# Residues of gate columns by VectorE in two blocks, and one more plain unit ahead of a pair in two places, in a hybrid attention/convolution block with SwiGLU

## The chip, the cores and the metric

The kernel runs on one core of one Trainium2 chip. The metric is device time in microseconds (us) of one execution, the median of several runs. Times inside an execution come from a hardware profile of one execution; they count from the start of its span.

The engines are TensorE (PE, matrix products; its weight loads are listed apart as PEld), VectorE (DVE), ScalarE (ACT), GpSimd (POOL) and SyncE (SP). SP does nothing here but issue loads; POOL issues the DMAs that add to what lies at their target.

## The reference, cut to what matters

All is float32, 256 tokens, width 2048, hidden width of the feed-forward part 5632.

```python
xn = rms_norm(h, norm1_g[l])
proj = jnp.einsum('bsd,dn->bsn', xn, w_in[l].astype(xn.dtype))
...
h = h + jnp.einsum('bsm,md->bsd', mixed, w_out[l].astype(mixed.dtype))
hn = rms_norm(h, norm2_g[l])
a = jnp.einsum('bsd,df->bsf', hn, w_gate[l].astype(hn.dtype))
bu = jnp.einsum('bsd,df->bsf', hn, w_up[l].astype(hn.dtype))
h = h + jnp.einsum('bsf,fd->bsd', jax.nn.silu(a) * bu, w_down[l].astype(hn.dtype))
```

What is left out (differential attention and a causal depthwise convolution with its norms) runs in the first 300 us and isn't touched. The change lies in the last three lines.

## The kernel before

**Products in three parts.** A float32 product is made of rounded halves: each operand is split into a rounded value (hi) and its residue (lo), and hi·hi, lo·hi and hi·lo are added up. For a weight tile `raw` that means a cast `whi` on ScalarE (L322) and a residue `wlo = raw - whi`. The residue is made in one of two ways. On VectorE it is one subtraction (L331). By DMA, ScalarE writes the negated rounded value to `wlo` (L325), and POOL issues a transfer that adds `raw` to it in place (L326), 512 KB each.

**Blocks and passes.** The hidden width is cut into 11 column blocks of 512 (j = 0 to 10), in groups of 4, 4 and 3. Behind each group comes a pass of `w_down` over the group's rows, as two double columns of 2 x 512. So the order is: block 0, blocks 1 to 3, pass; blocks 4 to 7, pass; blocks 8 to 10, pass. Block 0 is done plainly. Every other block, and every double column of a pass, is a list of units that share eight PSUM banks:

- **g** and **u**, plain units: two 128-row tiles of the gate (or up) columns, 12 matmuls of 128x512. In a pass, g and u are the left and right columns of a double column. First half: eight matmuls with `whi` (L1011, L1012). Second half: four with `wlo` (L1017).
- **s**, a pair: two row tiles of both gate and up columns as a 2x2 block product with seven products instead of eight, so 21 matmuls (L990, L991, L992). Its sums of weights are made on VectorE (L963, L964, L965), rounded on ScalarE (L966, L969), and the residues come from VectorE (`wlb` L972, `wlt` L973). The first L992 of a pair reads `wlt`, which is made last.

A block has four pairs and four units each of g and u. `BY_DMA` names the plain units whose residue is made by DMA: the first two g and the second and fourth u of a block. Block 1 has none of the g.

**Order.** A string gives each block's units: `ORDER` for blocks 2 to 10, `FIRST_ORDER` for block 1, `DORDERS` for the passes (by the number of blocks in the group, one string for each double column). `run_chunks` walks through the units. Near a pair it loads and rounds a unit three units ahead of TensorE, makes its residue two ahead, and loads a pair's weights six ahead. Everything else (sums of the banks L1091 to L1096, adding up a finished block or pass L1110 and L1151, transposes) is a generator that is taken one step further at fixed points within the units. So an engine's queue is fixed when the program is built, and each engine works strictly in that order; moving one letter of a string moves work on every engine.

Buffers: five of `raw`, three each of `whi` and `wlo`, two of a pair's weights `wb`. A load is issued by SP in the order of the program and waits there for its buffer, and what is behind it waits too.

**Names.** Below, "the first pair of block 4" is the first s of its string. Block 1 runs from 393.5 to 437 us, block 4 from 605.9 to 650.6, block 8 from 861.2 to 906.3, the last double column of the last pass from 1022.2 to the end.

Of the kernel before, what the change touches and what calls it, by code (L numbers as in the profile page):

```python
# [77 lines left out]
BY_DMA = dict(g=TWOS[:2], u=TWOS[1::2])  # L78

ORDER = "sggsggsuusuu"  # L80
FIRST_ORDER = "gsgsggsuusuu"


HD = N // P
ND = 2
DORDERS = {4: ("gguuggsguugsuu", "sgggugggusuuuu"), 3: ("gguusggsuu", "ggsggsuuuu")}

Q1, Q6, Q7, Q5, Q2, Q4, Q3, QX = range(8)

# [7 lines left out]
FIRSTS = [sum(FGROUPS[: g + 1]) for g in range(len(FGROUPS))]  # L97
# [13 lines left out]
def tile_block(  # L111
# [925 lines left out]
    def fast_block(order, pairs, twos, sources, operands, half, whole, by_dma=dict(g=(), u=())):  # L1037

        units, sums = [], {}
        left = dict(s=list(pairs), g=list(twos), u=list(twos))  # L1040
        for kind in order:
            what = left[kind].pop(0)
            c = dict(kind=kind, sums=sums, done=None, first={}, last={}, rows=what["rows"], **operands)
            if kind == "s":
                c.update(p=what["p"], load=lambda c: None, round=round_pair, split=split_pair, multiply=multiply_pair,
                         uses=[q for q, _, _ in PRODUCTS])
                c["from"] = sources
            else:
                w, col = sources[kind]
                c.update(ks=what["ks"], w=w, nk=2, width=N, cols=[(col, N)], by_dma=what["k"] in by_dma[kind],  # L1050
                         load=load_chunk, round=round_chunk, split=split_chunk, multiply=multiply_two,
                         uses=(Q3, QX) if kind == "u" else (Q2, Q4))
            units.append(c)
        assert not any(left.values())
        for q in range(8):
            users = [c for c in units if q in c["uses"]]
            users[0]["first"][q] = users[-1]["last"][q] = True
        [c for c in units if c["kind"] != "u"][-1]["done"] = half
        units[-1].update(done=whole, prompt=True)
        chunks.extend(units)  # L1060

    def gate_up_block(j):
        fast_block(ORDER if j > 1 else FIRST_ORDER, [dict(p=p, rows=slice(p, p + HK + 1, HK)) for p in range(NS)],
                   [dict(ks=ks, rows=slice(ks[0], ks[1] + 1, ks[1] - ks[0]), k=ks) for ks in TWOS],
                   dict(g=(w_gate, j * N), u=(w_up, j * N)),
                   dict(pairs=lambda: forms.get("pair"), plain=lambda k: forms["plain"][k]),
                   products_done, lambda sums: block_done(j, sums),
                   BY_DMA if j > 1 else dict(g=(), u=BY_DMA["u"]))

    def down_pass(g, j0, nb):  # L1070
        k0 = j0 * HD
# [2 lines left out]
                for a, b in zip(ks[::2], ks[1::2])]  # L1074
        for i, order in enumerate(DORDERS[nb]):
            n = 2 * i
# [28 lines left out]
    def block_done(j, q):  # L1105
        while "g" not in halfway:
            yield
        g, u = halfway.pop("g"), halfway.pop("u")
        for m, i in enumerate((Q3, QX)):
            dve.tensor_tensor(u[m], q[i], u[m], ALU.add)  # L1110
        for m in range(NM):
            dve.tensor_tensor(u[m], u[m], g[m], ALU.mult)
        yield from lag(4)
        yield from transposed(j, u)
# [74 lines left out]
    for g, nb in enumerate(FGROUPS):  # L1189
        for j in range(j0, j0 + nb):  # L1190
            if j:
                gate_up_block(j)
                continue

            block(w_gate, j * N, range(KD), fh, silu_done)
            block(w_up, j * N, range(KD), fh, lambda ps, j=j: up_done(j, ps))
            chunks[-1]["prompt"] = True
        down_pass(g, j0, nb)
        j0 += nb
# [33 lines left out]
```

## Time and profile before

| | us |
|---|---|
| median of three runs (lowest, highest) | 1063.49 (1062.6, 1063.9) |
| the profiled execution's own time | 1060.47 |
| its span | 1058.7 |
| share of the chain of work that ended last: TensorE, VectorE, DMA | 83%, 7%, 3% |

By stretch of the span, the busy time of each engine, the granted clock and the mean busy share of the 16 DMA engines (block 4 and block 8 are the first and third row, the blocks behind them the second and fourth):

```profile
606.00:656.00 50.00, 46.78 (x208) 38.05 (x207) 41.44 (x41) 28.85 (x26) 6.28 (x8) 1.00 0.98 280
656.00:698.00 42.00, 42.00 (x191) 34.77 (x190) 37.68 (x36) 27.79 (x26) 3.47 (x4) 1.00 0.83 250
861.00:911.00 50.00, 47.56 (x203) 38.90 (x202) 41.22 (x40) 29.14 (x26) 6.60 (x8) 0.97 0.98 280
911.00:954.00 43.00, 43.00 (x198) 35.60 (x196) 38.67 (x37) 28.19 (x27) 3.46 (x4) 1.00 0.83 247
```

The columns behind the stretch are its length and the busy us of PE, PEld, DVE, ACT and POOL, each with its number of instructions, then clock, DMA share and GB/s. In the two blocks that come first in a group TensorE has idle time and the DMA engines have hardly any; in the blocks behind them it is the other way round.

### The profile page before, as it was taken

How to read it: one execution, taken by the hardware profiler on the slowest of the kernel's cores; microseconds unless marked ns; L12 is line 12 of the kernel's file. 1: busy time of each engine (PE TensorE's matmuls, PEld its weight loads, DVE VectorE, ACT ScalarE, POOL GpSimd, SP SyncE). 2: the span in 40 equal slices, each digit the busy share in tenths (PEclk: the TensorE clock that was granted, in tenths of full speed). 3: DMA queues.
4: the chain of work that ended last, by engine and by line, in shares of the span. 5: the costliest groups of instructions: out<-in, count | busy, mean ns of one | idle time of the engine just before them, and what ended most of it. 6: DMA issues, size and time to landing. Idle time of an engine off the chain costs nothing.

```text
span 1058.7 us, 13117 instructions
## 1 busy us (share of the span) xinstructions
PE 1042.8 (99%) x4702; PEld 857.3 (81%) x4702; DVE 892.2 (84%) x1087; ACT 626.3 (59%) x802; POOL 104.5 (10%) x147
## 2 busy tenths in 40 slices
PE   9999999999999999999999989999999999999998
PEld 7888888877888777888888878888888878888876
DVE  5799989899666699899687888989878788889896
ACT  6644567755766565676453656666654456667442
POOL 0030122211100100000001100000000110010010
PEclk9999999999999999999999999999999999999999
DMA  9755555553546566987857698879856889798692
GB/s 300 232 179 194 199 171 171 176 170 133 176 171 226 183 228 205 292 254 223 250 186 226 202 293 246 266 207 277 259 172 226 237 209 295 211 296 251 173 280 95
DMA packets 123470, 231.33 MB, mean 219 GB/s; under 512 B 7956, under 2 KB 25806, under 8 KB 123404
## 3 DMA queue, kind: packets, MB, share of 16 engines
q1 hardware_dynamic: 113904, 201.61, 56.3%
q0 software_dynamic: 9440, 28.84, 14.0%
q8 instruction: 37, 0.61, 0.2%
q14 instruction: 29, 0.24, 0.1%
q10 hardware_dynamic: 60, 0.03, 0.0%
HBM read 202.14 MB, written 9.44 MB: 200 GB/s over the span
## 4 chain that ended last, share of the span: by engine, by line
PE 83%; DVE 7%; DMA 3%; issue 3%; ACT 2%; POOL 2%; DVEq 0%; POOLq 0%; ACTq 0%
PE q L1017 11%; PE q L1011 11%; PE q L1012 11%; PE acc L367 9%; PE acc L362 9%; PE acc L361 9%; PE q L992 7%; PE q L990 7%; PE q L991 7%; DVE wlo L331 2%; DMA wlo<-raw 2%; DVE y L512 1%; PE ps_a L828 1%; ACT whi L322 1%; PE ps_o L724 1%
## 5 line engine op out<-in xcount | busy, mean ns | idle before, releaser
L322 ACT CAST whi<-raw 128x1024 fp32r<-128x1024 f32 x272 | 282.6, 1051 | 162.9 <-PE acc L362 56.7
L331 DVE TENSOR_TENSOR wlo<-raw,whi 128x1024 fp32r<-128x1024 f32 x234 | 283.7, 1225 | 87.5 <-ACT whi L322 85.6
L969 ACT CAST wh<-wt 128x2048 fp32r<-128x2048 f32 x52 | 99.6, 1915 | 63.4 <-DVE wt L965 62.9
L973 DVE TENSOR_TENSOR wlt<-wt,wh 128x2048 fp32r<-128x2048 f32 x52 | 119.1, 2290 | 15.0 <-ACT wh L969 14.7
L361 PE MATMUL acc<-whi,xhi 128*128 128x512 f32 x320 | 126.3, 395 | 0.5 <-ACT whi L322 0.5
L1011 PE MATMUL q<-whi,chi 128*128 128x512 f32 x320 | 125.7, 393 | 0.0
L362 PE MATMUL acc<-whi,xlo 128*128 128x512 f32 x320 | 125.0, 391 | 0.2 <-DVE xlo L236 0.2
L1012 PE MATMUL q<-whi,clo 128*128 128x512 f32 x320 | 124.8, 390 | 0.0
L990 PE MATMUL q<-wh,fhi 128*128 128x512 f32 x280 | 109.9, 393 | 0.0
L991 PE MATMUL q<-wh,flo 128*128 128x512 f32 x280 | 109.0, 389 | 0.0
L512 DVE SCALAR_TENSOR_TENSOR y<-upad,cw,y 128x256 f32<-128x256 f32 x240 | 102.8, 490 | 0.0
L1011 PE MATMUL q<-whi,ahi 128*128 128x512 f32 x256 | 100.2, 391 | 0.0
L1012 PE MATMUL q<-whi,alo 128*128 128x512 f32 x256 | 99.7, 389 | 0.0
L972 DVE TENSOR_TENSOR wlb<-wb,wh 128x1536 fp32r<-128x1536 f32 x52 | 91.1, 1753 | 5.3 <-ACT wh L966 5.3
L1017 PE MATMUL q<-wlo,chi 128*128 128x512 f32 x320 | 86.8, 393 | 5.7 <-DMA wlo<-raw 5.7
L367 PE MATMUL acc<-wlo,xhi 128*128 128x512 f32 x320 | 87.7, 396 | 0.9 <-DVE wlo L331 0.8
L966 ACT CAST wh<-wb 128x1536 fp32r<-128x1536 f32 x52 | 76.7, 1474 | 0.0
L1017 PEld LDWEIGHTS q<-wlo,chi 128*128 128x128 f32 x320 | 60.3, 189 | 19.3 <-DMA wlo<-raw 6.9
L326 POOL DMA_DIRECT2D wlo<-raw x38 | 32.8, 864 | 402.0 <-ACT wlo L325 209.5
L361 PEld LDWEIGHTS acc<-whi,xhi 128*128 128x128 f32 x320 | 60.1, 188 | 13.5 <-ACT whi L322 0.8
L362 PEld LDWEIGHTS acc<-whi,xlo 128*128 128x128 f32 x320 | 60.1, 188 | 13.2 <-DVE xlo L236 1.0
L1011 PEld LDWEIGHTS q<-whi,chi 128*128 128x128 f32 x320 | 60.4, 189 | 12.5
(229 smaller groups left out, 1782.4 us busy)
## 6 DMA issues: line engine op xcount, KB each, us to landing
raw<-in_w_down_dram SPq DMA_DIRECT2D x64, 512.0 KB, 7.4
raw<-in_w_in_dram SPq DMA_DIRECT2D x48, 512.0 KB, 4.6
raw<-in_w_gate_dram SPq DMA_DIRECT2D x48, 512.0 KB, 7.2
raw<-in_w_up_dram SPq DMA_DIRECT2D x48, 512.0 KB, 6.4
wb<-in_w_up_dram SPq DMA_DIRECT2D x40, 512.0 KB, 3.8
wb<-in_w_gate_dram SPq DMA_DIRECT2D x40, 512.0 KB, 5.0
wlo<-raw POOLq DMA_DIRECT2D x38, 512.0 KB, 6.8
raw<-in_w_in_dram SPq DMA_DIRECT2D x64, 256.0 KB, 5.6
```

The source lines that it names most:

```text
L322: act.copy(c["hi"], c["raw"])
L331: dve.tensor_tensor(c["lo"], c["raw"], c["hi"].bitcast(F32), ALU.subtract)
L361: pe.matmul(ps[m], xhi[:, ms], hi[:, j, :], start=c["first"] and j == 0, stop=False)
L362: pe.matmul(ps[m], xlo[:, ms], hi[:, j, :], start=False, stop=False)
L367: pe.matmul(ps[m], xhi[:, ms], lo[:, j, :], start=False, stop=c["last"] and j == nk - 1)
L512: dve.scalar_tensor_tensor(y[:, ct, :], src, wk, y[:, ct, :], ALU.mult, ALU.add)
L973: dve.tensor_tensor(lot, c["t"], c["hi"][:, :SUMMED].bitcast(F32), ALU.subtract)
L990: pe.matmul(ps, hi, c["hi"][:, w], start=bool(first), stop=False)
L991: pe.matmul(ps, lo, c["hi"][:, w], start=False, stop=False)
L1011: pe.matmul(ps, xs[i][0][:, ms], hi[:, i, :], start=i == 0 and bool(c["first"].get(qs[m])), stop=False)
L1012: pe.matmul(ps, xs[i][1][:, ms], hi[:, i, :], start=False, stop=False)
L1017: pe.matmul(sum_bank(c, qs[m]), xs[i][0][:, ms], lo[:, i, :], start=False, stop=i == 1 and bool(c["last"].get(qs[m])))
```

## The change

Three edits. The g units of the first block behind a pass (blocks 4 and 8; `FIRSTS` holds 4, 8 and 11) get their residues from VectorE instead of DMA. In block 1 the third g moves ahead of the second pair. In the second double column of the last pass the third g moves ahead of the first pair.

```diff
-FIRST_ORDER = "gsgsggsuusuu"
+FIRST_ORDER = "gsggsgsuusuu"
...
-DORDERS = {4: ("gguuggsguugsuu", "sgggugggusuuuu"), 3: ("gguusggsuu", "ggsggsuuuu")}
+DORDERS = {4: ("gguuggsguugsuu", "sgggugggusuuuu"), 3: ("gguusggsuu", "gggsgsuuuu")}
...
-                   BY_DMA if j > 1 else dict(g=(), u=BY_DMA["u"]))
+                   BY_DMA if j > 1 and j not in FIRSTS else dict(g=(), u=BY_DMA["u"]))
```

VectorE's queue at the start of block 4, from the last up unit's residue of the pass on, before:

```order
L331 TENSOR_TENSOR wlo<-raw,whi 128x1024
L972 TENSOR_TENSOR wlb<-wb,wh 128x1536
L973 TENSOR_TENSOR wlt<-wt,wh 128x2048
L1151 TENSOR_TENSOR sum_5407<-q_5209,sum_5407 128x512
L1151 TENSOR_TENSOR sum_5409<-q_5274,sum_5409 128x512
L963 TENSOR_TENSOR wt<-wb 128x1024
L964 TENSOR_TENSOR wt<-wb,wt 128x512
L965 TENSOR_TENSOR wt<-wt,wb 128x512
L972 TENSOR_TENSOR wlb<-wb,wh 128x1536
L973 TENSOR_TENSOR wlt<-wt,wh 128x2048
```

and of the change:

```order
L331 TENSOR_TENSOR wlo<-raw,whi 128x1024
L972 TENSOR_TENSOR wlb<-wb,wh 128x1536
L973 TENSOR_TENSOR wlt<-wt,wh 128x2048
L331 TENSOR_TENSOR wlo<-raw,whi 128x1024
L1151 TENSOR_TENSOR sum_5407<-q_5209,sum_5407 128x512
L1151 TENSOR_TENSOR sum_5409<-q_5274,sum_5409 128x512
L331 TENSOR_TENSOR wlo<-raw,whi 128x1024
L963 TENSOR_TENSOR wt<-wb 128x1024
L964 TENSOR_TENSOR wt<-wb,wt 128x512
L965 TENSOR_TENSOR wt<-wt,wb 128x512
L972 TENSOR_TENSOR wlb<-wb,wh 128x1536
L973 TENSOR_TENSOR wlt<-wt,wh 128x2048
```

The two new L331 stand on either side of the pass's last sums, and the second pair's work (L963 to the last L973) is behind both. At the same place ScalarE loses two L325 and POOL two L326. Block 8 reads alike.

VectorE's queue in block 1, from behind block 0's products (the second and third pair are the two groups of L963 to L973), before:

```order
L331 TENSOR_TENSOR wlo<-raw,whi 128x1024
L963 TENSOR_TENSOR wt<-wb 128x1024
L964 TENSOR_TENSOR wt<-wb,wt 128x512
L965 TENSOR_TENSOR wt<-wt,wb 128x512
L972 TENSOR_TENSOR wlb<-wb,wh 128x1536
L973 TENSOR_TENSOR wlt<-wt,wh 128x2048
L331 TENSOR_TENSOR wlo<-raw,whi 128x1024 x2
L963 TENSOR_TENSOR wt<-wb 128x1024
```

and of the change:

```order
L331 TENSOR_TENSOR wlo<-raw,whi 128x1024 x2
L963 TENSOR_TENSOR wt<-wb 128x1024
L964 TENSOR_TENSOR wt<-wb,wt 128x512
L965 TENSOR_TENSOR wt<-wt,wb 128x512
L972 TENSOR_TENSOR wlb<-wb,wh 128x1536
L973 TENSOR_TENSOR wlt<-wt,wh 128x2048
L331 TENSOR_TENSOR wlo<-raw,whi 128x1024
L963 TENSOR_TENSOR wt<-wb 128x1024
```

One residue moved from behind the second pair to in front of it. On TensorE a whole plain unit and a group of four transposes (L828) moved in front of that pair; on SP one load of gate weights moved ahead of its `wb`.

VectorE's queue at the start of the last double column (the L1096 belongs to the one before; the first pair is L963 to the first L973), before:

```order
L1096 TENSOR_TENSOR sum_8654<-q_8443,sum_8654 128x512
L963 TENSOR_TENSOR wt<-wb 128x1024
L964 TENSOR_TENSOR wt<-wb,wt 128x512
L965 TENSOR_TENSOR wt<-wt,wb 128x512
L331 TENSOR_TENSOR wlo<-raw,whi 128x1024
L1151 TENSOR_TENSOR sum_8653<-q_8498,sum_8653 128x512
L1151 TENSOR_TENSOR sum_8655<-q_8501,sum_8655 128x512
L972 TENSOR_TENSOR wlb<-wb,wh 128x1536
L973 TENSOR_TENSOR wlt<-wt,wh 128x2048
L331 TENSOR_TENSOR wlo<-raw,whi 128x1024 x2
L963 TENSOR_TENSOR wt<-wb 128x1024
```

and of the change:

```order
L1096 TENSOR_TENSOR sum_8650<-q_8439,sum_8650 128x512
L331 TENSOR_TENSOR wlo<-raw,whi 128x1024
L1151 TENSOR_TENSOR sum_8649<-q_8494,sum_8649 128x512
L1151 TENSOR_TENSOR sum_8651<-q_8497,sum_8651 128x512
L963 TENSOR_TENSOR wt<-wb 128x1024
L964 TENSOR_TENSOR wt<-wb,wt 128x512
L965 TENSOR_TENSOR wt<-wt,wb 128x512
L331 TENSOR_TENSOR wlo<-raw,whi 128x1024
L972 TENSOR_TENSOR wlb<-wb,wh 128x1536
L973 TENSOR_TENSOR wlt<-wt,wh 128x2048
L331 TENSOR_TENSOR wlo<-raw,whi 128x1024
L963 TENSOR_TENSOR wt<-wb 128x1024
```

The first pair's work moved behind the two L1151, which add the last sums of the double column before; the second pair now follows with one residue between them instead of two.

## The prediction, made before the changed kernel ran

> **What bounds the kernel now.** First the page, for the engine that sets the time, then the view of waits of that engine:
>
> ```profile
> PE 1042.8 (99%) x4702; PEld 857.3 (81%) x4702; DVE 892.2 (84%) x1087; ACT 626.3 (59%) x802; POOL 104.5 (10%) x147
> ```
> ```profile
> PE q L1017 <- DMA wlo<-raw: 5.7, 3, 3.0
> PE q L992 <- DVE wlt L973: 1.9, 2, 1.0
> ```
>
> TensorE is busy 99% of the span, and nothing in the change alters what it multiplies. So the only time to be had is what TensorE spends waiting or running slowly. The two largest entries are the two that the change aims at: a plain unit's third products (L1017) waiting for a residue made by DMA, and a pair's third matmul (L992) waiting for VectorE. The timeline of TensorE shows where. Block 4 (columns: start, length, both us; the bracket is idle time before and who ended it):
>
> ```profile
> 610.70 0.39 PE L1011 MATMUL q<-whi,chi 128*128 128x512 f32 x1
> ...
> 615.71 1.20 PE L1017 MATMUL q<-wlo,chi 128*128 128x512 f32 x4 [3.03 <-DMA wlo<-raw]
> ...
> 619.94 0.39 PE L990 MATMUL q<-wh,fhi 128*128 128x512 f32 x1
> ```
>
> Block 8:
>
> ```profile
> 866.04 0.39 PE L1011 MATMUL q<-whi,chi 128*128 128x512 f32 x1
> ...
> 870.46 2.07 PE L1017 MATMUL q<-wlo,chi 128*128 128x512 f32 x4 [2.44 <-DMA wlo<-raw]
> ...
> 875.71 0.39 PE L990 MATMUL q<-wh,fhi 128*128 128x512 f32 x1
> ```
>
> The second pair of block 1, and the last pass:
>
> ```profile
> 404.57 0.39 PE L990 MATMUL q<-wh,fhi 128*128 128x512 f32 x1
> 404.79 0.39 PE L991 MATMUL q<-wh,flo 128*128 128x512 f32 x1
> 406.21 0.50 PE L992 MATMUL q<-wlt,fhi 128*128 128x512 f32 x1 [1.03 <-DVE wlt L973]
> 406.55 0.40 PE L990 MATMUL q<-wh,fhi 128*128 128x512 f32 x1
> ```
> ```profile
> 1027.63 0.39 PE L990 MATMUL q<-wh,dhi 128*128 128x512 f32 x1
> 1027.86 0.39 PE L991 MATMUL q<-wh,dlo 128*128 128x512 f32 x1
> 1029.13 0.50 PE L992 MATMUL q<-wlt,dhi 128*128 128x512 f32 x1 [0.88 <-DVE wlt L973]
> ...
> 1033.57 0.39 PE L1011 MATMUL q<-whi,ahi 128*128 128x512 f32 x1
> ...
> 1039.01 0.39 PE L990 MATMUL q<-wh,dhi 128*128 128x512 f32 x1
> ```
>
> Undisturbed matmuls start 0.227 us apart. The last two rows give a yardstick: two plain units take 1039.01 - 1033.57 = 5.44 us, so one takes 2.72 (first half 1.81, second 0.91), and a pair (21 matmuls) about 4.77. A pair wants its first residue 0.45 us after its start.
>
> **Blocks 4 and 8: the residues.** What goes is, in each block, two negated casts on ScalarE (L325) and two accumulating transfers of 512 KB. What comes is two subtractions (L331) on VectorE. Between the start of the first gate unit and the next pair block 4 takes 619.94 - 610.70 = 9.24 us, block 8 875.71 - 866.04 = 9.67 us. At the yardstick both take 5.44. So **3.80 us** and **4.23 us** are to be had, if nothing else is late.
>
> Part of the second sum is clock. Behind a wait of 2.44 us four matmuls took 2.07 us, where the four behind the longer wait of block 4 took 1.20. The unit's eighth matmul started at 866.04 + 7 x 0.227 = 867.63, so the wait itself is 870.46 - 867.63 less one step, 2.6 us. The other 1.6 us are that half speed. The Trainium skill ("TensorE: Matmul & The Clock Gate", Part 1) states that the array drops to half clock after an idle window of about 3.4 us and that the window runs freely. Here the gap of 2.44 us was followed by half speed and that of 3.03 us was not, so length alone does not decide. I take the trace (one of two), with none and both as bounds: 1.6 us either way.
>
> Is anything else late? VectorE's queue in block 4:
>
> ```profile
> 603.82 2.28 DVE L973 TENSOR_TENSOR wlt<-wt,wh 128x2048 fp32r<-128x2048 f32 x1
> 606.02 1.28 DVE L1151 TENSOR_TENSOR sum<-q,sum 128x512 f32<-128x512 f32 x2
> 607.22 1.21 DVE L963 TENSOR_TENSOR wt<-wb 128x1024 f32<-128x1024 f32 x1
> ...
> 611.87 2.29 DVE L973 TENSOR_TENSOR wlt<-wt,wh 128x2048 fp32r<-128x2048 f32 x1 [0.31 <-ACT wh L969]
> ```
>
> The new L331 of the first gate unit runs at 606.02, where L1151 stood; its rounded half was cast before (ScalarE loses work here). It is done by 607.2; TensorE wants it at 610.70 + 1.81 = 612.5. The second runs behind L1151, done by 609.6, wanted at 615.2. Neither is waited for. What queues behind them is the second pair: L963, L964, L965, ScalarE's cast L969, L973. An L331 takes 1.13 us of the queue (1023.92 - 1022.79 in the rows of the last pass, below), so all of it moves by 2.27 us: L973 ends at 611.87 + 2.29 + 2.27 = 616.43. The pair now starts at 610.70 + 5.44 = 616.14 and wants it at 616.59. **Margin 0.16 us**: I cost it at nothing; the bound is 0.4 us a block, should the casts or the semaphores come a little later. Block 8 is the same picture with the same margin: its L973 ended at 869.50, becomes 871.77, wanted at 866.04 + 5.44 + 0.45 = 871.93.
>
> ```profile
> 867.21 2.29 DVE L973 TENSOR_TENSOR wlt<-wt,wh 128x2048 fp32r<-128x2048 f32 x1 [0.31 <-ACT wh L969]
> ```
>
> The third pair is freer. Its chain follows the second's end by two L331 and 6.94 us (L963's start to L973's end, 607.22 to 614.16): 616.3 + 2.27 + 6.94 = 625.5, wanted at 616.14 + 4.77 + 5.44 + 0.45 = 626.8. That holds if the fourth gate unit's weights land by 616; the DMA view from 600 to 660 us speaks for it:
>
> ```profile
> q0 software_dynamic: 1424, 4.16, 37.4%
> ```
>
> The queue with the accumulating transfers took 37.4% of 60 us on all 16 engines for 4.16 MB, 5.4 us a MB. Two residues are 1.05 MB: 5.6 us of all engines go from the busiest stretch.
>
> SP's queue moves too: the fourth pair's weights are issued when L972 of the second is done, now 2.27 us later, and the first two up units' behind them. More on that among the rivals.
>
> **Block 1: a plain unit in front of the second pair.** TensorE wanted L992 at 404.57 + 0.45 = 405.02 and had it at 406.21; the next step was 0.34 instead of 0.227. Together **1.30 us**. Afterwards the pair starts one unit (2.72) and one group of transposes later, while the extra L331 in front of its chain costs 1.13, so its residue is there at 406.15 + 1.13 = 407.3, wanted after 407.7. The third pair's chain hardly moves, as the L331 only changed sides and L839 now stands behind it: its L973 ends near 415.3, wanted near 415.7. L992 of the first pair still waits its 0.2 us. On SP a gate load is now ahead of the second pair's weights and holds them until its buffer is free; they are used some 8 us later. I cost these at nothing, bound 0.3.
>
> **The last pass: three gate units first.** Here VectorE is the bound, and the gain is not the whole wait:
>
> ```profile
> 1020.21 1.22 DVE L963 TENSOR_TENSOR wt<-wb 128x1024 f32<-128x1024 f32 x1
> ...
> 1022.79 1.22 DVE L331 TENSOR_TENSOR wlo<-raw,whi 128x1024 fp32r<-128x1024 f32 x1
> 1023.92 1.28 DVE L1151 TENSOR_TENSOR sum<-q,sum 128x512 f32<-128x512 f32 x2
> 1025.12 1.75 DVE L972 TENSOR_TENSOR wlb<-wb,wh 128x1536 fp32r<-128x1536 f32 x1
> 1026.79 2.29 DVE L973 TENSOR_TENSOR wlt<-wt,wh 128x2048 fp32r<-128x2048 f32 x1
> 1028.99 2.35 DVE L331 TENSOR_TENSOR wlo<-raw,whi 128x1024 fp32r<-128x1024 f32 x2
> ```
>
> The two L1151 now stand ahead of the pair's L963, and they wait for TensorE's last unit of the pass before. That unit ends where the first gate unit starts, 1027.63 - 5.44 = 1022.19; its four third products start at 1021.28, and the first sum is complete after two of them: 1021.28 + 0.23 + 0.39 = 1021.9. From there: two L1151 (1.20), L963 to L965 (1022.79 - 1020.21 = 2.58), L331 (1.13), L972 (1026.79 - 1025.12 = 1.67), L973 (2.29): 1021.95 + 8.87 = 1030.82. The pair now starts at 1027.63 + 2.72 = 1030.35 and wants it at 1030.80: a wait of about 0.1 us with the slow step, so it ends near 1030.87 + 4.44 = 1035.3 (4.44 as from 1029.13 to 1033.57). The next pair follows after one unit only: start 1038.0, wanted at 1038.5. Its chain is L973's slot (1028.99 - 1026.79 = 2.20), one L331 (1.13) and 6.94 us behind 1028.54: 1038.8. Wait 0.4 us, with the slow step 0.5. It ends at 1038.85 + 4.44 = 1043.3, against 1039.01 + 4.77 = 1043.8 before. **0.5 us** gained of 1.15; bounds 0 and 1.15. Behind it the same four up units follow.
>
> **Sum.** 3.8 + 4.2 + 1.3 + 0.5 = 9.8 us off the profiled execution: span 1058.7 to 1048.9, its own time 1060.47 to 1050.7. The median of the runs shown is 1063.49, 3.0 us more than that execution; the same difference gives 1053.7 us.
>
> **Rivals.** (1) The clock: typical runs may not have the half-speed stretch, as block 4 had none. Then 1.6 us of the sum do not exist: 1055.3. For it: only one wait of the two had it. By the free-running window of the Trainium skill ("TensorE: Matmul & The Clock Gate", Part 1) it would be a matter of chance in each run. Chance 0.18.
>
> (2) The wait moves to the next residue by DMA, the second up unit's. TensorE wants that at 616.14 + 4.77 + 5.44 + 4.77 + 2.72 + 1.81 = 635.7 now. Its DMA can be issued only when ScalarE has cast it, behind the third pair's L969: by my estimate near 626.6. Landing times of the four residues from 600 to 640 us:
>
> ```profile
> DMA to landing us min/median/max: 5.8/8.3/11.7
> ```
>
> At the median it lands at 634.9, at the longest at 638.3: a wait of 2.6 us. Twice that is 5.2: 1058.9. Against it: the long ones are the two that go. Chance 0.10.
>
> (3) The change swaps one wait for another: VectorE's chain comes not 0.2 but several us late at the second and third pairs of blocks 4 and 8. It would need about 2 us at each of the four to bring the gain under 0.2% (2.1 us), and the queue worked out above has that only if L969's cast were delayed as well. Time 1062. Chance 0.04.
>
> (4) Slower: SP's queue. The first two up units' weights were issued from here on, now 2.27 us later:
>
> ```profile
> 612.57 3.48 SPq L317 DMA_DIRECT2D raw<-in_w_up_dram  x2
> ```
>
> The first must be cast before TensorE reaches it at 631.1, so it must land by 630, 15.2 us after an issue at 614.8. Each us beyond is lost in both blocks. The time passes 1063.49 + 2.1 when landing takes over 21 us, 1.8 times the longest above; at 22 us it is 1067.3. Chance 0.03.
>
> **How the numbers follow.** Forecast 0.65, rivals 0.18, 0.10, 0.04, 0.03. Low end: half speed behind both waits (-1.6), the last pass in full (-0.65), and 1 us for the three that the runs take beyond the profiled one: 1050.5. High end: no half speed (+1.6), nothing in the last pass (+0.5), both blocks' bound (+0.8), block 1's (+0.3), and some of rival 2: 1057.5. Against 0.2%, about what a measurement of this kernel can tell from no change, faster has 0.93, same 0.04, slower 0.03.
>
> **What would show it.** In the changed profile the waits of L1017 for DMA should be gone; blocks 4 and 8 should take 5.4 to 5.9 us from the first gate unit to the second pair; L992 of block 1's second pair should not wait; in the last pass both pairs should wait, together about half a microsecond. The forecast is wrong if L992 waits over 0.5 us in blocks 4 or 8, or if L1017 waits for the up unit's residue.

## The result, and the profile after

| | before | changed |
|---|---|---|
| median of the runs (lowest, highest), us | 1063.05 (1062.09, 1063.9) | 1051.05 (1050.87, 1051.5) |
| the profiled execution's own time, us | 1060.47 | 1051.14 |
| its span, us | 1058.7 | 1049.4 |

The ratio is 0.9888, with a 95% interval of 0.9871 to 0.9905: 12.0 us gained, 1053.7 us forecast, 1051.05 measured. The changed kernel's four runs lie within 0.6 us of each other, those of before within 1.8.

The view of TensorE's waits from 380 us on (who waited for whom; us in total, times, longest) has one row left:

```profile
PE q L992 <- DVE wlt L973: 0.2, 1, 0.2
```

The waits for a residue by DMA are gone. The timeline of TensorE at the first gate unit and the second pair of block 4, and of block 8 (start, length, us):

```profile
609.42 0.39 PE L1011 MATMUL q<-whi,chi 128*128 128x512 f32 x1
...
614.86 0.39 PE L990 MATMUL q<-wh,fhi 128*128 128x512 f32 x1
615.09 0.39 PE L991 MATMUL q<-wh,flo 128*128 128x512 f32 x1
615.32 0.39 PE L992 MATMUL q<-wlt,fhi 128*128 128x512 f32 x1
```
```profile
861.20 0.39 PE L1011 MATMUL q<-whi,chi 128*128 128x512 f32 x1
...
866.64 0.39 PE L990 MATMUL q<-wh,fhi 128*128 128x512 f32 x1
866.86 0.39 PE L991 MATMUL q<-wh,flo 128*128 128x512 f32 x1
867.09 0.44 PE L992 MATMUL q<-wlt,fhi 128*128 128x512 f32 x1
```

Both stretches take 5.44 us, in place of 9.24 and 9.67. VectorE's queue in block 4 with the two new L331 to either side of L1151:

```profile
602.54 2.28 DVE L973 TENSOR_TENSOR wlt<-wt,wh 128x2048 fp32r<-128x2048 f32 x1
604.75 1.22 DVE L331 TENSOR_TENSOR wlo<-raw,whi 128x1024 fp32r<-128x1024 f32 x1
605.88 1.28 DVE L1151 TENSOR_TENSOR sum<-q,sum 128x512 f32<-128x512 f32 x2
607.08 1.22 DVE L331 TENSOR_TENSOR wlo<-raw,whi 128x1024 fp32r<-128x1024 f32 x1
608.21 1.22 DVE L963 TENSOR_TENSOR wt<-wb 128x1024 f32<-128x1024 f32 x1
...
612.87 2.29 DVE L973 TENSOR_TENSOR wlt<-wt,wh 128x2048 fp32r<-128x2048 f32 x1 [0.32 <-ACT wh L969]
```

L973 ends at 615.16 and TensorE reads it at 615.32: the margin of 0.16 us is there, and no more. By stretch (columns as in the table of before), the two blocks now keep TensorE busy throughout, VectorE works 45.9 us of 50, and the DMA engines are no longer full:

```profile
604.00:654.00 50.00, 50.00 (x224) 41.23 (x223) 45.89 (x44) 30.67 (x27) 5.20 (x6) 1.00 0.90 265
859.00:909.00 50.00, 50.00 (x224) 41.25 (x223) 45.99 (x42) 32.02 (x28) 4.94 (x6) 1.00 0.90 268
```

In the last double column VectorE is still what TensorE waits for, now mainly at the second pair:

```profile
1021.36 0.39 PE L990 MATMUL q<-wh,dhi 128*128 128x512 f32 x1
1021.58 0.39 PE L991 MATMUL q<-wh,dlo 128*128 128x512 f32 x1
1021.88 0.50 PE L992 MATMUL q<-wlt,dhi 128*128 128x512 f32 x1
...
1029.88 0.50 PE L992 MATMUL q<-wlt,dhi 128*128 128x512 f32 x1 [0.22 <-DVE wlt L973]
```

An undisturbed pair reads `wlt` 0.45 us after its start; the first does so after 0.52, the second (start 1029.04) after 0.84.

### The profile page after: what moved, and what is told of

It reads as the page before. It is cut to its first block, busy times and chain, and to the rows that moved or that the text cites. A ratio compares the mean times of both kernels' runs of the same rounds, so it can differ in the third digit from the quotient of the medians.

```text
span 1049.4 us, 13104 instructions
## 1 busy us (share of the span) xinstructions
PE 1040.1 (99%) x4702; PEld 855.9 (82%) x4702; DVE 896.4 (85%) x1091; ACT 622.1 (59%) x798; POOL 99.3 (9%) x143
## 4 chain that ended last, share of the span: by engine, by line
PE 62%; DVE 2%; DMA 1%; ACT 0%; issue 0%; DVEq 0%
PE q L1017 12%; PE q L1011 12%; PE q L1012 12%; PE q L992 8%; PE q L990 8%; PE q L991 8%; PE ps_a L828 1%; DMA raw<-in_w_down_dram 1%; PE acc L367 1%; PE acc L361 1%; PE acc L362 1%; DVE wlo L331 1%; DVE wlt L973 0%; DVE wt L963 0%; ACT wh L969 0%
## 5 line engine op out<-in xcount | busy, mean ns | idle before, releaser
L331 DVE TENSOR_TENSOR wlo<-raw,whi 128x1024 fp32r<-128x1024 f32 x238 | 288.3, 1224 | 82.2 <-ACT whi L322 82.1
L973 DVE TENSOR_TENSOR wlt<-wt,wh 128x2048 fp32r<-128x2048 f32 x52 | 119.1, 2290 | 14.7 <-ACT wh L969 14.5
L1017 PE MATMUL q<-wlo,chi 128*128 128x512 f32 x320 | 85.8, 390 | 0.0
L1017 PEld LDWEIGHTS q<-wlo,chi 128*128 128x128 f32 x320 | 59.9, 188 | 13.1 <-DMA wlo<-raw 0.7
L367 PEld LDWEIGHTS acc<-wlo,xhi 128*128 128x128 f32 x320 | 59.3, 188 | 13.6 <-DVE wlo L331 1.8
L1012 PEld LDWEIGHTS q<-whi,clo 128*128 128x128 f32 x320 | 60.1, 188 | 12.3
```

The costliest lines, as they stand in the source:

```text
L331: dve.tensor_tensor(c["lo"], c["raw"], c["hi"].bitcast(F32), ALU.subtract)
L367: pe.matmul(ps[m], xhi[:, ms], lo[:, j, :], start=False, stop=c["last"] and j == nk - 1)
L973: dve.tensor_tensor(lot, c["t"], c["hi"][:, :SUMMED].bitcast(F32), ALU.subtract)
L1012: pe.matmul(ps, xs[i][1][:, ms], hi[:, i, :], start=False, stop=False)
L1017: pe.matmul(sum_bank(c, qs[m]), xs[i][0][:, ms], lo[:, i, :], start=False, stop=i == 1 and bool(c["last"].get(qs[m])))
```

## Experiments

**1 and 2. The kernel before, twice more.** The first question is where the 2.2 us lie by which the gain is larger than forecast.

> The kernel before, unaltered, for a second profile. The change measured 12.0 us, and the first profile of before accounts for 9.8. Theory A: the waits for the residues in blocks 4 and 8 are longer, or followed by half speed more often, in most executions than in the profiled one: from the first gate unit to the second pair the two blocks together take over 20 us here (18.9 in the first profile), and the execution is over 1061 us. Theory B: the waits are the same in every execution and the missing 2.2 us lie elsewhere: 18.9 us again within 0.5, whatever the execution's time.

Measured: 1062.28 us, span 1060.4. From the first gate unit to the second pair block 4 took 12.16 us and block 8 8.53, together 20.69. The timeline of TensorE in block 4 of this execution, with all that lies between the wait and the next pair:

```profile
616.24 2.08 PE L1017 MATMUL q<-wlo,chi 128*128 128x512 f32 x4 [3.56 <-DMA wlo<-raw]
618.11 0.63 PE L1011 MATMUL q<-whi,chi 128*128 128x512 f32 x1
...
621.10 0.63 PE L1012 MATMUL q<-whi,clo 128*128 128x512 f32 x1
621.52 1.51 PE L1017 MATMUL q<-wlo,chi 128*128 128x512 f32 x4
622.87 0.39 PE L990 MATMUL q<-wh,fhi 128*128 128x512 f32 x1
```

and in block 8:

```profile
873.15 1.21 PE L1017 MATMUL q<-wlo,chi 128*128 128x512 f32 x4 [2.26 <-DMA wlo<-raw]
874.20 0.40 PE L1011 MATMUL q<-whi,chi 128*128 128x512 f32 x1
```

The half speed is behind the other wait this time, and lasts longer: matmuls of 0.63 us, 0.43 apart, through the whole second gate unit, so late that its own residue is there before it is wanted.

> The kernel before once more, for a third profile. With the waits and the half speed behind them as the part that varies (theory A), its span less the two stretches from the first gate unit to the second pair of blocks 4 and 8 is 1039.7 to 1040.0 us, as in the first two profiles (1058.7 - 18.9 and 1060.4 - 20.7); if something else varies, that difference moves by more than half a microsecond.

Measured: 1061.79 us, span 1059.9, the two stretches 9.89 and 9.62 us. The rest of the span is 1040.4 us, against 1039.8 and 1039.7 in the other two: 0.6 to 0.7 us more, beyond the half microsecond allowed, so something else varies as well. It lies ahead of the blocks: the same matmul at the end of block 0 starts at 387.25 here and at 386.56 and 386.57 in the others. Theory A holds for the blocks; the start of the program varies too, by some 0.7 us.

The granted clock of every run says more than these three profiles. Of the 23 runs of the kernel before on the chip of items 1 and 3 to 5, the one with a mean clock of 1.000 took 1059.05 us, the two with 0.998 took 1060.07 and 1060.29, the fifteen with 0.997 between 1061.43 and 1062.41, and the four with 0.995 between 1063.06 and 1063.74. The execution that the prediction worked from had 0.998; the changed kernel's four runs had 0.999 or 1.000. A mean clock lower by 0.005 stands for 5.3 us of 1060. So time at half clock is most of what varies in the kernel before.

**3 to 5. Each edit alone.** The diffs are the three pieces of the change, one at a time.

```diff
-                   BY_DMA if j > 1 else dict(g=(), u=BY_DMA["u"]))
+                   BY_DMA if j > 1 and j not in FIRSTS else dict(g=(), u=BY_DMA["u"]))
```

> Only the residues of blocks 4 and 8 move to VectorE; both order strings as before. If the gain lies in those residues: 8.0 us by the first profile of before, 10 us if typical executions lose more there (theory A), so 1053 to 1055 us against 1063. If it is the orders that carry it (rival): under 3 us.

Measured: 1053.04 us, ratio 0.9919 [0.9906, 0.9931]; both stretches 5.44 us. 8.9 us of the gain are in this edit.

```diff
-FIRST_ORDER = "gsgsggsuusuu"
+FIRST_ORDER = "gsggsgsuusuu"
```

> Only the string of block 1 as in the change. Forecast term: 1.3 us (the wait of the second pair's L992 goes). Rival: the first pair or the first up unit's DMA residue takes the wait over, gain 0 to 0.5 us. If the two waits in blocks 4 and 8 vary from run to run, this is hardly to be told from no change by its time, and its profile decides.

Measured: 1060.27 us against 1061.99, ratio 0.9985 [0.9977, 0.9994]. From the second gate unit's start to the third pair's block 1 took 14.73 us before and takes 13.42 here and in the change: the 1.3 us, and no wait took its place.

```diff
-DORDERS = {4: ("gguuggsguugsuu", "sgggugggusuuuu"), 3: ("gguusggsuu", "ggsggsuuuu")}
+DORDERS = {4: ("gguuggsguugsuu", "sgggugggusuuuu"), 3: ("gguusggsuu", "gggsgsuuuu")}
```

> Only the string of the last double column as in the change. Forecast term: 0.5 us, both pairs waiting for VectorE, 0.1 and 0.4 to 0.5 us, in place of 1.15 us at the first. Rival: the whole 1.15 us goes. The time alone will not tell; the profile's waits of L992 will.

Measured: 1061.04 us, ratio 0.9992 [0.9983, 1.0002]: by its time no difference. In its profile the pairs take 5.00 and 5.28 us to the next unit, in place of 5.93 and 4.76: 0.41 us gained, and the wait of the first pair is mostly handed on to the second, as worked out.

**6 and 7. Is it the wait for the residue, or the crowding by its transfers?** The changed kernel, with the removed transfers put back where nobody reads them:

```diff
+        if c.get("idle"):
+            pool.dma_start(out=c["view"](aside.pop()), in_=c["raw"], accum_op=ALU.add)
...
+        for t in aside:
+            sp.dma_start(out=t, in_=w_gate[:P, : NK * N])
```

> The change, and in blocks 4 and 8 two accumulating transfers of 512 KB again from the same two weight tiles at the same places of POOL's queue, but into a tile in device memory that nobody reads (four loads of 512 KB at the start give it its first values). Theory 1: what TensorE lost was the wait for those residues, and half speed behind it. Then the stretch from the first gate unit to the second pair stays at 5.4 to 6 us in both blocks and the time at 1050 to 1053 us; the first two up units of these blocks may wait a little, since their loads come later. Rival: it was the crowding of the DMA engines by these transfers, whoever reads them. Then the two stretches go back over 7.5 us each, or the next loads make TensorE wait as long, and the time is 1056 us or more.

Measured: 1061.46 us, ratio 0.9994 [0.9985, 1.0002], which looks like the rival. The profile shows that most of it is an accident of the experiment: the four loads that give `aside` its values delay everything from the start, and the end of block 0 comes 6.9 us later than in the change (393.48 against 386.54). So it was made again with those loads spread over the projections:

```diff
+    for i, t in enumerate(aside):
+        before[48 + 10 * i] = lambda t=t: pool.dma_start(out=t, in_=w_gate[:P, : NK * N])
```

> The run with the unread transfers again, but their target in device memory is given its first values by four transfers spread over the projections, since four loads at the start delayed everything behind them by 6.9 us in the last run. Theory 1 (the wait for a residue that TensorE reads): blocks 4 and 8 take 5.4 us to the second pair, and wait only at the third pair, whose plain units are loaded late, for about 1.5 us each; the time is 1053 to 1056 us. Rival (the crowding itself costs as much): 1058 us or more.

Measured: 1055.07 us, ratio 0.9943 [0.9931, 0.9956], on the chip where the change alone had 1051.19 (below). Both stretches to the second pair take 5.44 us. TensorE waits at the third pair of both blocks instead, and once 0.5 us for a later residue by DMA (line numbers are 6 higher in this kernel: L998 and L979 are the L992 and L973 of the others):

```profile
625.09 0.50 PE L996 MATMUL q<-wh,fhi 128*128 128x512 f32 x1
625.42 0.40 PE L997 MATMUL q<-wh,flo 128*128 128x512 f32 x1
627.41 0.73 PE L998 MATMUL q<-wlt,fhi 128*128 128x512 f32 x1 [1.59 <-DVE wlt L979]
```

ScalarE and VectorE at that place show why:

```profile
616.86 1.05 ACT L326 CAST whi<-raw 128x1024 fp32r<-128x1024 f32 x1 [4.25 <-DMA raw<-in_w_gate_dram]
618.19 1.05 ACT L326 CAST whi<-raw 128x1024 fp32r<-128x1024 f32 x1 [0.28 <-DMA raw<-in_w_gate_dram]
```
```profile
617.94 2.56 DVE L337 TENSOR_TENSOR wlo<-raw,whi 128x1024 fp32r<-128x1024 f32 x2 [3.01 <-ACT whi L326]
620.42 1.22 DVE L969 TENSOR_TENSOR wt<-wb 128x1024 f32<-128x1024 f32 x1
```

The third and fourth gate units' weights land after 616 us. They are not issued later: SP issues these two loads at 603.91 us and in the change at 603.58, but here they take 13.6 us to land, there 6.4 (median of the two). VectorE stands idle for 3 us, and the third pair's work is behind those units' residues in its queue. In the change the same casts run without a wait:

```profile
612.74 2.00 ACT L322 CAST whi<-raw 128x1024 fp32r<-128x1024 f32 x2
```

So both theories have a part. Of the 10.6 us that the change gains on this chip (1061.77 to 1051.19), 6.7 are there with the transfers running. This kernel has the two altered strings as well, which account for about 1.8 of them (1.3 and 0.5, items 4 and 5 and the steps below). That leaves about 4.9 us for the wait for the residue itself, half speed included. 3.9 us come back with the crowding alone, and by this other way, through late weights. In the kernel before this second loss was there to be had, too, but lay hidden: the weights of the fourth gate unit came late there as well, while TensorE was held up by the residue. The split holds for transfers into device memory, which this run used; the ones before went into on-chip memory, and were issued some 6 us later.

**8. One residue by DMA left in.**

```diff
-                   BY_DMA if j > 1 and j not in FIRSTS else dict(g=(), u=BY_DMA["u"]))
+                   BY_DMA if j > 1 and j not in FIRSTS else dict(g=BY_DMA["g"][1:] if j > 1 else (), u=BY_DMA["u"]))
```

Only in blocks 4 and 8 the second gate unit's residue is made by DMA; the first goes to VectorE, and all else is as in the change.

> The change, but in blocks 4 and 8 the second gate unit's residue goes by DMA again and only the first's by VectorE. Theory 1a: two such transfers at once were the trouble, one is in time: issued near 605, landing by 613 to 615, wanted at 614. No wait over 0.5 us, the second pair's residue 1.1 us earlier than in the change, the time 1050.5 to 1052. Rival 1b: in this stretch even one comes too late: L1017 of the second gate unit waits 1 to 3 us in each block, with half speed behind the wait in some executions, and the time is 1053 to 1058.

Measured: 1052.4 us (1051.33 to 1052.78), ratio 0.9903 [0.9888, 0.9918] on its own chip, where the change gave 0.9888 and 0.9906 on two others; the time does not tell it from the change. Its profile (span 1051.0) does. The waits of TensorE from 380 us on, and block 4:

```profile
PE q L1017 <- DMA wlo<-raw: 1.0, 1, 1.0
PE q L992 <- DVE wlt L973: 0.2, 1, 0.2
```
```profile
615.64 1.20 PE L1017 MATMUL q<-wlo,chi 128*128 128x512 f32 x4 [1.02 <-DMA wlo<-raw]
616.68 0.39 PE L990 MATMUL q<-wh,fhi 128*128 128x512 f32 x1
```

One transfer alone is late by 1.0 us in block 4 and hardly at all in block 8 (5.67 us from the first gate unit to the second pair, against 5.44), and no half speed follows. The long waits of before were for the first unit's residue; the second unit reads its own 2.72 us later, and that is most of what the first one lacked. Being alone did not make this transfer much quicker: in block 4 TensorE starts on it 10.1 us after its issue (605.52 to 615.64), and on the first one of before 10.4 us after (605.31 to 615.71). A single residue by DMA, for the second unit, is just about as late as it may be, and the second pair then has more room: L973 ends some 1.1 us earlier and the pair starts later, a margin of 2.6 us in block 4. The change has spent that margin down to 0.16 us to be rid of the last microsecond.

**9 and 10. What the change leaves.** Two strings altered further, and the change beside it on the same chip:

```diff
-FIRST_ORDER = "gsggsgsuusuu"
+FIRST_ORDER = "ggsgsgsuusuu"
...
-DORDERS = {4: ("gguuggsguugsuu", "sgggugggusuuuu"), 3: ("gguusggsuu", "gggsgsuuuu")}
+DORDERS = {4: ("gguuggsguugsuu", "sgggugggusuuuu"), 3: ("gguusggsuu", "gggsgusuuu")}
```

In block 1 the two plain units come together at the start; in the last double column one more plain unit goes between its first and second pair.

> The change with two strings altered further: block 1 begins with two gate units (ggsgsgsuusuu), and in the last double column one up unit stands between the third gate unit's pair partner and the last pair (gggsgusuuu). Theory: the waits of L992 that the change leaves (0.2 us with its slow step at block 1's first pair, about 0.4 us with it at the last pair) go, the tail is no longer, and 0.5 to 0.9 us are gained on the change: span near 1048.7, time near 1050.4. Rival: VectorE's chain is as long as before, so the wait only moves to the next pair, and with three up units in place of four behind the last pair the final sums become the last thing: no gain, or up to 1 us lost.

Measured: 1050.69 us (1050.41 to 1050.99), ratio 0.9891 [0.9877, 0.9904]. Block 1 takes 21.35 us from its first gate unit to its third pair, 21.70 in the change; the last double column 31.07 us from its first unit to its last matmuls, 31.55 in the change. That is 0.8 us less. In this execution's span only 0.3 of it is seen (1049.1 against 1049.4), since the same matmul at the end of block 0 came 0.46 us later (387.00 against 386.54). To see how far the change's own time varies, both were run side by side:

> The changed kernel once more, on the same chip as the next one. 1050.5 to 1051.5 us if its executions vary as little as in the first four (0.6 us), as they should with no wait left that depends on when a transfer lands.

> The version with both strings altered further, on the same chip as the change. Its profile has no wait of L992 left; so 0.5 to 0.9 us less than the change, if nothing at the end takes it back; if the tail grew, no difference.

Measured: the change 1051.19 us (1050.99 to 1052.64), ratio 0.9906 [0.9893, 0.992]; with both strings altered 1050.62 us (1050.29 to 1051.59), ratio 0.9897 [0.9882, 0.9912]. The altered strings gain 0.57 us by the medians, but the intervals overlap, and each kernel has one run a microsecond above its others. The change's run at 1052.64 is outside what was expected of it. The version with both strings has the lowest medians of all kernels here, and is not told apart from the change by its times. Its profile is of its run at 1051.59, and shows one place where such a microsecond can come from, in the pass behind block 7, which no edit touches:

```profile
840.69 0.39 PE L990 MATMUL q<-wh,dhi 128*128 128x512 f32 x1
841.97 0.50 PE L992 MATMUL q<-wlt,dhi 128*128 128x512 f32 x1 [0.66 <-DVE wlt L973]
```

The same matmul in the changed kernel's first profile:

```profile
840.80 0.39 PE L990 MATMUL q<-wh,dhi 128*128 128x512 f32 x1
841.25 0.39 PE L992 MATMUL q<-wlt,dhi 128*128 128x512 f32 x1
```

There it starts an undisturbed 0.45 us after its pair, here after 1.28, in the change's second profile after 0.74, with the first edit alone with a wait of 0.36. What differs is when the weights of the pass land. ScalarE's queue just ahead, in the version with both strings:

```profile
828.55 1.05 ACT L322 CAST whi<-raw 128x1024 fp32r<-128x1024 f32 x1 [3.83 <-DMA raw<-in_w_down_dram]
832.01 2.23 ACT L322 CAST whi<-raw 128x1024 fp32r<-128x1024 f32 x2 [2.40 <-DMA raw<-in_w_down_dram]
```

In the change's first profile the two waits were 2.98 and 2.21 us. What makes those loads land later in one execution than in another was not tried.

## Why the prediction was right, point by point

**The waits for DMA residues in blocks 4 and 8.** Forecast: both stretches at 5.44 us, no other wait in their place. Measured: 5.44 and 5.44, in the change and with this edit alone. The close steps came out as worked out from VectorE's queue. The margin of the second pair was forecast as 0.16 us in both blocks; it is 0.16 in block 4, and 0.11 in block 8 (L973 ends at 866.98, L992 starts at 867.09). In the third pair of block 4 it was forecast as 1.3 (625.5 against 626.8) and is 1.26 (624.29 against 625.55).

**Block 1.** Forecast 1.30 us, measured 14.73 - 13.42 = 1.31. The second pair's residue, forecast for 407.3, was there at 407.29.

**The last pass.** Forecast 0.5 us, with a wait handed on to the second pair. Measured 21.58 - 21.12 = 0.46 from the first unit to the first up unit in the change and 0.41 alone, and the wait was handed on.

**The mis-sized term.** The forecast of 1053.7 is 2.65 us too long: 0.44 because the kernel before ran in 1063.05 and not 1063.49, and 2.2 because 12.0 us were gained in place of 9.8. The steps themselves came to 9.8 as measured too: 3.80 and 4.23 in blocks 4 and 8, 1.31 and 0.46. The profiled span fell by 9.3, half a microsecond less, lost in small differences elsewhere. The term that was off is "3.8 + 4.2" for the residues, as a measure of typical runs. It came from one execution, and that was one of the better ones. Five executions with all the residues by DMA (before, its two repeats, and the two kernels with only the other edits) lost, against 10.88 undisturbed, in blocks 4 and 8 together:

| | before | before, item 1 | before, item 2 | item 4 | item 5 |
|---|---|---|---|---|---|
| two stretches, us | 18.91 | 20.69 | 19.51 | 19.49 | 21.77 |
| lost, us | 8.0 | 9.8 | 8.6 | 8.6 | 10.9 |

The mean is 9.2 us, 1.2 more than the forecast used. With it the sum is 11.0 us, between the 12.0 measured on the first chip and the 10.6 on the chip of item 7; that these two differ by 1.4 us is not explained, the start of the program alone varies by 0.7. The prediction took the 3.0 us by which the runs lay above the profiled execution and added them to the changed kernel's time as they stood. Most of them was the very loss that the edit takes away, and belonged in the gain: the change's own profiled execution took 1051.14 us against the 1050.7 forecast for it, and its median, 1051.05, lies no higher. The range held with 0.55 us to spare, by the 1.6 us that its low end allowed for half speed behind both waits.

**The rivals.** (1), no half speed in typical runs, had the wrong sign: half speed followed in six of the ten waits of the five executions, and in one of these executions in both. (2), a wait for the next residue, the up unit's, did not come: no profile of the change has a wait at L1017. (3), VectorE several microseconds late, did not come either, as the margins show. (4), loads that land too late, did not come in the change. With the removed transfers put back (item 7) late weights did cost TensorE a wait and a half-speed stretch, by way of gate units and VectorE rather than up units, so its place was wrong but late weights are a real danger here.

**What the prediction had no term for.** It gave 5.6 us of DMA time as support for the third pair's margin, and charged nothing for it. Item 7 puts 3.9 us on it, of the some 8.8 that the residues' edit gains: with the same transfers still running, and nobody waiting for them, the third pair waits. In the forecast that sits inside the assumption "if the fourth gate unit's weights land by 616". The assumption held in the change, and its price was unnamed.

## What to carry to other kernels

When a wait is removed, walk down the queue of the engine that takes the work over and compare each chunk's end with the moment at which it is wanted; with durations from the trace, margins as small as 0.1 us came out right here. If the wait came from a transfer, ask also which loads were late because of that transfer while the wait hid them: in item 7, removing the waiting alone left 3.9 of some 8.8 us behind. And where the runs lie above the profiled execution, suspect that what varies is the loss that the edit removes, and widen the gain, not only the time.

## What the runs showed of the hardware that was not expected

**Half speed behind a wait is not decided by the wait's length.** Behind some waits matmuls start 0.43 us apart in place of 0.227, which costs 1.5 to 3.0 us in all. It followed waits of 2.44, 2.51, 2.59, 3.46, 3.55 and 3.56 us, and did not follow waits of 2.26, 2.32, 3.03 and 3.62. Behind two of them (2.59 and 3.55) it began only 1.3 us after the wait had ended. It also followed the 1.59 us of item 7:

```profile
628.37 0.63 PE L997 MATMUL q<-wh,flo 128*128 128x512 f32 x1
628.79 0.63 PE L998 MATMUL q<-wlt,fhi 128*128 128x512 f32 x1
...
630.92 0.40 PE L997 MATMUL q<-wh,flo 128*128 128x512 f32 x1
631.17 0.40 PE L998 MATMUL q<-wlt,fhi 128*128 128x512 f32 x1
```

What matters is where a wait falls. In the blocks of these profiles the clock is granted at half for 3.41 us, or for twice that, and then in full again, and all such stretches of one execution lie on one grid of 3.41 us: in the kernel of item 5 one ends at 622.11 us and the next begins at 874.70, 74 such windows later. Two windows at block 8 of the kernel before, two at block 4 of its second repeat, item 2, counted back by whole windows from its stretch at half, which begins at 871.30 (columns as in the table of before; the last but two is the granted clock):

```profile
866.88:870.29 3.41, 1.13 (x6) 0.59 (x4) 3.10 (x3) 1.24 (x2) 0.00 (x0) 1.00 1.07 252
870.30:873.71 3.41, 3.25 (x8) 2.58 (x9) 0.63 (x2) 1.37 (x2) 0.00 (x0) 0.50 1.06 245
```
```profile
611.89:615.30 3.41, 1.48 (x7) 0.90 (x5) 3.10 (x3) 1.59 (x2) 0.00 (x0) 1.00 1.05 246
615.30:618.71 3.41, 1.72 (x7) 1.42 (x8) 0.69 (x1) 0.06 (x1) 0.00 (x0) 1.00 1.06 246
```

The wait of 2.44 us left TensorE 1.13 us of work in one window, and the next window had half the clock (0.50). The wait of 3.62 us was cut in two by the edge of a window, TensorE had 1.48 and 1.72 us of work on the two sides, and the clock stayed full. In blocks 4 and 8 of the five executions, half the clock followed each of the six windows at full clock with 1.36 us of work or less, and none with 1.48 or more. Item 7 does not fit this border: its window had 1.78 us of work (624.10 to 627.51), and half the clock followed. So the border is not fully known.

The Trainium skill ("TensorE: Matmul & The Clock Gate", Part 1) gives an idle window of about 3.4 us for the drop. The trace agrees on the window's length, 3.41 us, but the window need not be idle throughout: up to 1.36 us of work in it, and once 1.78, did not prevent the drop. For costing, a wait of 1.6 us or more may double in price, by the chance of where it falls.

**Adding transfers are dear.** In the kernel before, from 600 to 660 us, they moved 4.16 MB in 37.4% of 60 us, 5.4 us of all 16 engines for a MB. The plain loads of the whole program moved 201.6 MB in 56.3% of the span:

```profile
q1 hardware_dynamic: 113904, 201.61, 56.3%
```

That is 3.0 us for a MB, and in the 60 us of the first figure it was the same (11.03 MB in 54.3%). So an add by DMA of 512 KB costs about as much DMA time as 0.9 MB of loads, beside the loads that it delays.
